# Mixer of layer 0: from a hand-braided order to recording and list scheduling

## The chip, the cores and the metric

The kernel runs on one core of a Trainium2 chip. The metric is the device time of one execution in microseconds (us), lower is better; several executions are timed and the median stands. One further execution is recorded by the hardware profiler, and every row below is of that one.

## The reference, cut to what matters

A decoder trunk of two layers over 16 learned tokens followed by 1024 tokens of width 1024, in float32. Layer 0 mixes with an RWKV-7 recurrence beside a causal pooling; layer 1 with differential attention. The change is in layer 0's mixer.

```python
def rwkv_pool_mixer(h, w_in, ...):            # layer 0
    y = h @ w_in                              # 18 slices of 128 columns here
    ys = ys + (prev - ys) * mu                # shift by one token
    r, k, v, wd, ad, gd = split(ys)
    decay, a, g = ...                         # low-rank products of wd, ad, gd
    o = rwkv7_scan(r, decay, k, v, kk, a)     # 8 heads: S = S*w + sa kk' + v k',  o = S r
    o = (groupnorm(o) * ln_w + ln_b + bonus) * g
    z = pooled differences of u, times pool_w # 4 groups, windows 2, 4, 8, 16
    return concatenate([o, z]) @ w_out

for i in range(2):
    m = rwkv_pool_mixer(hn) if i == 0 else diff_attn_mixer(hn)
    h = h + rmsnorm(m, g[1])
    h = h + rmsnorm(sq_relu_mlp(rmsnorm(h, g[2])), g[3])
```

## The kernel before, in words

**Layout.** Channels lie on the 128 partitions, tokens along the free axis. Large products are done in three TensorE passes on a high and a low part of each operand (`mm3`, L217 to L219: high by high, low by high, high by low). The small matrices of the recurrence are plain float32.

**The pieces of mixer 0.** Two heads make a pair, so there are four pairs p = 0 to 3. The scan is done in 17 chunks of 64 tokens, one alone and then eight groups of two: nine groups for each pair.
- `project` (L1009 to L1024) makes one of 18 slices of the input projection, and writes it to memory (`yd`, L1015) through a queue.
- `prep` (L1138 to L1180) loads a pair's slices back (`yl`, `la`) and builds the operands of each chunk: `pk` in memory, `ldd` (the triangular part) and a bonus `bond`.
- `invert` (L1190 to L1219) inverts the unit triangular blocks of a pair, 68 of 32 x 32 at once: loads `li` from `ldd`, then 31 steps of two VectorE operations each (L1211, L1212, on `li`, `xi`, `tm`), then `xi` goes out to `xd` (L1215) and comes back as `ds` (L1218, L1219).
- `chain` runs the recurrence over the nine groups of a pair, each group from the state that the one before left. Per group: load `lt` from `pk` (L1234), masks on GpSimd (`bd`, L1236, L1239), float32 matmuls (L1244, L1248, L1252, L1259, L1260, L1270, L1271, L1274, L1276), ScalarE and VectorE between them. Each 256 or so columns of output are finished by `fin` (L1287 to L1296): a norm (one matmul, L1290), scales, a product on GpSimd (L1295), and a store to `ozd`, from which `loads` (L1334, split on L237 and L238) brings them back as operands of the output projection.
- `pool_group` (L1306 to L1327) is the pooling of one channel group.
- `early` (matmul triples into `pse`) is the part of the output projection (6 of its 8 weight slices) that only needs finished operands.
- `late` (L537 and others) is the rest of layer 0: remaining output projection, norm, MLP. It is a list of tasks that a scheduler, class `Flow`, puts in order.

**What sets the order.** Mixer 0 is written in seven stages (`PLAN`, L60); in a stage `braid` takes pieces from several generators in turn, at fixed rates. Each engine executes its instructions in that order and waits where an operand isn't there. Nearly all of the mixer's transfers are issued by one queue, SP, in the same order: one that waits holds all behind it. `Flow` knows a cost for each task, its engine, what it needs, and one shared memory bus; it ranks tasks by the longest path behind them and places at each step the one that can start soonest. Before, only `late` and the stages behind it are ordered so.

**Buffers.** Pools give out tiles in rotation: PSUM has two banks for `project` and `early`, two for the chain's products (`xs`, `qp`), one each for `prep`'s results (`sa`, `sb` share one), its norms, the chain's output `ob` and its state `sp`. `li` and `xi` have one buffer each; the state S three; `ft` in `fin` five; `yl` five.

The names that follow have the kernel's own lines.

Of the kernel before, what the change touches and what calls it, by code (L numbers as in the profile page):

```python
# [7 lines left out]
F32 = mybir.dt.float32  # L8
# [53 lines left out]

class Later:
# [12 lines left out]
class Flow:  # L76
# [6 lines left out]
    def add(self, eng, cost, fn, r, w, port=False, size=0, tail=0.0):  # L83
# [8 lines left out]
        i = len(self.tasks)  # L92
        self.tasks.append((eng, cost, fn, deps, port, size, tail))
        for x in r:
            self.read.setdefault(x, set()).add(i)
        for x in w:
            self.wrote[x] = i
            self.read[x] = set()

# [65 lines left out]

class Trunk:
# [18 lines left out]
    def nm(self, s):  # L185
        self.uid += 1
        return f"{s}{self.uid}"

# [24 lines left out]
    def mm3(self, ps, ws, xs, first=True, last=True):  # L213
        nc = self.nc
        n = len(ws)
        for i, ((wh, wl), (xh, xl)) in enumerate(zip(ws, xs)):
            nc.tensor.matmul(ps, wh, xh, start=(first and i == 0), stop=False)  # L217
            nc.tensor.matmul(ps, wl, xh, start=False, stop=False)  # L218
            nc.tensor.matmul(ps, wh, xl, start=False, stop=(last and i == n - 1))  # L219
# [151 lines left out]
    def ahead(self, l):  # L371
# [5 lines left out]
        n = self.lw_n = (768, 768, 1024, 1024) if l == 0 else (640, 640, 1024, 1024, 1024)  # L377
# [15 lines left out]

    def late_weight(self, l, i, ne):
        nc = self.nc
        raw = self.R[0][:, i % 2, :self.lw_n[i]]
        hi, lo = self.lw(i)
        nc.sync.dma_start(raw, self.lw_src(l, i))
        nc.scalar.copy(hi, raw)
        nc.vector.tensor_tensor(lo, raw, hi.bitcast(F32), op=ALU.subtract)  # L400

    def late(self, l, xs, part, hin, hmid, hout, pre, rsb):
# [619 lines left out]
    def yload(self, mt, a, b):  # L1022
        y = self.yp.tile([P, 320], F32, tag="yl", name=self.nm("yl"), bufs=5)
# [93 lines left out]
    def prep_group(self, p, g0, m, e, ys, la, bo):  # L1117
# [45 lines left out]
        sb = self.mps.tile([P, 2, 4, C], F32, tag="p", name=self.nm("sb"))  # L1163
        for i in range(m):
            nc.tensor.matmul(sa[:, i, 2:4], kbd[:, i], w4[:, i, 1:3], start=True, stop=True)
        for i in range(m):
            nc.tensor.matmul(sa[:, i, 0:2], bbd[:, i], w4[:, i, 1:3], start=True, stop=True)
        for i in range(m):
# [3 lines left out]
        nc.vector.tensor_tensor(sg[:, :m, 0:4:2], sa[:, :m, 0:4:2],  # L1172
                                cb[:, None, None, B_MA:B_MA + C].broadcast_to([P, m, 2, C]), op=ALU.mult)
        nc.scalar.copy(sg[:, :m, 1:4:2], sa[:, :m, 1:4:2])
# [15 lines left out]
    def invert(self, p):  # L1190
# [3 lines left out]
        li = pp.tile([ni, 32, 32], F32, tag="li", name=self.nm("li"), bufs=1)  # L1194
        x = pp.tile([ni, 32, 32], F32, tag="xi", name=self.nm("xi"), bufs=1)
# [27 lines left out]
    def chain(self, p):  # L1223
# [5 lines left out]
        for f0, f1 in ((0, 1), (1, 5), (5, 9), (9, 13), (13, 17)):  # L1229
            ob = self.ops_.tile([P, 2, 4 * C], F32, tag="o", name=self.nm("ob"))  # L1230
            for g0 in range(f0, f1, 2):
# [33 lines left out]
                for i in range(n):  # L1265
# [3 lines left out]
                    if gi:  # L1269
# [605 lines left out]
```

## Time and profile before

| | us |
|---|---|
| median of 3 runs | 2822.95 (2817.04 to 2824.75) |
| the profiled execution | 2818.43 |
| its span, first to last instruction | 2816.6 |
| mixer 0 behind its entry and low-rank products, in the span | about 82 to 677 |
| mean granted TensorE clock over the span | 0.968 |

The profile's rows are of three kinds. Windows give the busy time of each engine in a stretch; matmuls overlap, so a busy TensorE isn't at its peak. A timeline lists instructions (neighbours that are alike are joined) with their start, their length and, in brackets, the idle time ahead of them and what ended it. The chain of waits follows the end of a stretch back to what released it.  PE is TensorE, PEld its weight loads, DVE VectorE, ACT ScalarE, POOL GpSimd, SP the queue for transfers, and SPq its issues. Kernel lines are written L1244.

Four instants cut mixer 0: the first matmul of each pair's chain (`xs<-lt,bd` of L1244, the single group of each pair). I call the stretches S0 (82 to chain 0), S1 (chain 0 to chain 1), S2 (chain 1 to chain 2), S3 (chain 2 to chain 3), S4 (chain 3 to the last `fin`), and "the tail" what lies between the last `fin` (L1290) and the long row of matmuls of `late`.

### The profile page before, as it was taken

Reading aid. Unit: us, or ns where it says so; the run is one execution under the profiler, and the core shown is the slowest. Engines: PE = TensorE matmul, PEld = TensorE weight load, DVE = VectorE, ACT = ScalarE, POOL = GpSimd, SP = SyncE. Lnnn points to the kernel's source line nnn. Section 1 sums busy time; section 2 is a strip of 40 time slices with the busy share of each in tenths; the row PEclk is TensorE's granted clock in tenths of the full one; section 3 lists DMA queues with packets and bytes.
Section 4 is the critical chain, followed back from the end, with each engine's and each line's share of the span. In section 5 each row is a group of like instructions: output and inputs, shape, how many; then the busy total and the mean of one; then the engine's idle time right before and its main releaser. Section 6 shows DMA issues by size and latency. Waiting matters only on the chain.

```text
span 2816.6 us, 44581 instructions
## 1 busy us (share of the span) xinstructions
PE 2622.5 (93%) x16822; PEld 2374.0 (84%) x16822; DVE 2102.9 (75%) x3889; ACT 1321.8 (47%) x2719; POOL 309.5 (11%) x404
## 2 busy tenths in 40 slices
PE   7999787898999999999968999999889999999997
PEld 6989786787899999999957898998786788878877
DVE  6568768463787778887795888878638787778888
ACT  6564564433643335433343556565635333344342
POOL 1112224131000000000012223222000000000000
PEclk9999988899999999999988999999999999999998
DMA  4656557555423346443342222222243233453443
GB/s 176 212 181 192 183 157 226 152 172 190 145 80 143 149 172 229 152 144 110 115 135 68 65 65 61 78 66 64 76 146 135 112 149 139 184 201 135 150 157 120
DMA packets 182774, 393.29 MB, mean 140 GB/s; under 512 B 43648, under 2 KB 106496, under 8 KB 170144
## 3 DMA queue, kind: packets, MB, share of 16 engines
q1 hardware_dynamic: 155376, 350.27, 37.4%
q10 hardware_dynamic: 27184, 40.18, 4.0%
q8 instruction: 132, 2.16, 0.3%
q14 instruction: 82, 0.67, 0.1%
HBM read 241.24 MB, written 132.24 MB: 133 GB/s over the span
## 4 chain that ended last, share of the span: by engine, by line
PE 63%; DVE 9%; ACT 2%; issue 2%; DMA 1%; POOL 0%; DVEq 0%; ACTq 0%; SPq 0%; POOLq 0%
PE bank L537 46%; PE psq L217 2%; PE psq L218 2%; PE psq L219 2%; PE s L1615 1%; PE tr L1661 1%; PE s L1617 1%; ACT p L1634 1%; PE pse L217 1%; PE bank L579 1%; PE av L1687 1%; PE pse L218 1%; PE pse L219 1%; DVE ac L614 1%; DVE p L1647 1%
## 5 line engine op out<-in xcount | busy, mean ns | idle before, releaser
L537 PE MATMUL bank<-opa,wp 128*128 128x260 f32 (+1 forms) x3296 | 655.4, 319 | 6.9 <-DVE wp L628 3.3
L537 PEld LDWEIGHTS bank<-opa,wp 128*128 128x128 f32 x3296 | 516.2, 188 | 56.7 <-DVE wp L628 5.0
L537 PE MATMUL bank<-opb,wp 128*128 128x260 f32 (+1 forms) x1150 | 347.6, 323 | 3.0 <-DVE ac L847 3.0
L537 PE MATMUL bank<-opa,hh 128*128 128x260 f32 (+1 forms) x1112 | 239.7, 320 | 7.2 <-DVE hh L628 5.3
L537 PEld LDWEIGHTS bank<-opb,wp 128*128 128x128 f32 x1150 | 216.3, 188 | 22.2 <-ACT opa L870 3.4
L847 DVE TENSOR_TENSOR ac<-bank,ac 128x520 f32<-128x520 f32 (+1 forms) x256 | 171.1, 691 | 67.5 <-PE bank L537 65.3
L537 PE MATMUL bank<-opa,opb 128*128 128x260 f32 (+4 forms) x1168 | 207.4, 308 | 13.4 <-ACT opb L516 7.1
L537 PEld LDWEIGHTS bank<-opa,hh 128*128 128x128 f32 x1112 | 184.8, 190 | 23.6 <-DVE hh L628 5.8
L537 PEld LDWEIGHTS bank<-opa,opb 128*128 128x128 f32 x1168 | 169.9, 196 | 24.9 <-ACT opb L516 7.5
L537 PE MATMUL bank<-opb,hh 128*128 128x260 f32 (+1 forms) x616 | 179.8, 325 | 0.0
L627 ACT CAST wp<-raw 128x512 fp32r<-128x512 f32 (+1 forms) x138 | 80.4, 584 | 199.3 <-PE bank L537 191.0
L627 ACT CAST wp<-ss 128x512 fp32r<-128x512 f32 (+1 forms) x130 | 76.5, 589 | 166.4 <-PE bank L537 141.1
L217 PE MATMUL ps<-opa,whi 128*128 128x346 f32 (+1 forms) x432 | 145.0, 336 | 0.4 <-DVE yt L1009 0.4
L218 PE MATMUL ps<-opa,wlo 128*128 128x346 f32 (+1 forms) x432 | 143.6, 332 | 0.0
L219 PE MATMUL ps<-opa,whi 128*128 128x346 f32 (+1 forms) x432 | 142.2, 329 | 0.6 <-DVE opa L315 0.6
L1634 ACT ACTIVATE p<-s,m 128x272 f32<-128x272 f32 (+7 forms) x128 | 95.6, 751 | 86.3 <-DVE m L1630 84.4
L537 PE MATMUL bank<-opa,tt 128*128 128x260 f32 (+1 forms) x648 | 130.5, 318 | 2.2 <-DVE ac L847 2.0
L537 PEld LDWEIGHTS bank<-opb,hh 128*128 128x128 f32 x616 | 116.9, 190 | 10.0
L217 PE MATMUL psq<-opa,wp 128*128 128x346 f32 (+2 forms) x352 | 118.1, 335 | 4.4 <-DVE rp L302 2.6
L203 POOL TENSOR_TENSOR wpx<-raw,wp 128x1024 fp32r<-128x1024 f32 (+1 forms) x14 | 33.9, 2425 | 789.8 <-PE bank L537 745.6
L219 PE MATMUL psq<-opa,wp 128*128 128x346 f32 (+2 forms) x352 | 113.8, 323 | 0.0
L537 PE MATMUL bank<-opb,opb 128*128 128x256 f32 (+4 forms) x456 | 111.4, 307 | 1.4 <-DVE tt L593 1.4
(408 smaller groups left out, 6928.2 us busy)
## 6 DMA issues: line engine op xcount, KB each, us to landing
raw<-in_w_dram SPq DMA_DIRECT2D x64, 1024.0 KB, 5.0
hid<-ac SPq DMA_DIRECT2D x14, 1820.0 KB, 6.6
hid<-ac SPq DMA_DIRECT2D x14, 1792.0 KB, 7.0
hh<-hid SPq DMA_DIRECT2D x23, 1040.0 KB, 5.1
hh<-hid SPq DMA_DIRECT2D x23, 1024.0 KB, 5.3
pk<-sg ACTq DMA_DIRECT2D x32, 704.0 KB, 4.4
lt<-pk SPq DMA_DIRECT2D x32, 704.0 KB, 4.6
raw<-in_w_qkv_dram SPq DMA_DIRECT2D x24, 512.0 KB, 3.4
```

The source lines that it names most:

```text
L203: (lo or nc.gpsimd).tensor_tensor(lw[:, :n], raw[:, :n], hi[:, :n].bitcast(F32), op=ALU.subtract)
L217: nc.tensor.matmul(ps, wh, xh, start=(first and i == 0), stop=False)
L218: nc.tensor.matmul(ps, wl, xh, start=False, stop=False)
L219: nc.tensor.matmul(ps, wh, xl, start=False, stop=(last and i == n - 1))
L537: nc.tensor.matmul(ps, use(x), use(y), start=start and i == j == 0, stop=i == len(ws) - 1 and j == 2, skip_group_check=not start)
L579: nc.tensor.matmul(acc, ones, use(src), start=first, stop=last)
L614: F.dve(NH, lambda mk=mk, k=k: stt(mk, mk, self.gcol(l, 1, k), y, op0=ALU.mult, op1=ALU.mult), r=nm + [("T", 2)], w=nm)
L627: F.act(n, lambda: nc.scalar.copy(use(t[0][:, :n]), src), r=rd, w=[z[0]] + claim)
L847: F.dve(NH, lambda d=d, q=q: tt(sv(d), q, sv(d), op=ALU.add), r=nq + nd, w=nd, ps=True)
L1615: nc.tensor.matmul(out(a, b), st[:, qs], kh[:, a:b], start=True, stop=False)
L1617: nc.tensor.matmul(out(a, b), st[:, qs], kl[:, a:b], start=False, stop=x1 <= x0)
L1634: nc.scalar.activation(p[:, :L0], S[c][:, :L0], AF.Exp, bias=m2[:, c:c + 1], scale=0.125, accum_out=m2[:, 2 + c:3 + c])
```

## The change

- Between the low-rank products and the end of mixer 0, `self.nc` is a `Recorder`: each call is kept with its engine, a cost, the memory regions that it reads and writes, and so its predecessors. At the end `rec.flow.run()` orders all with `Flow` and emits them. `PLAN` and `braid` still set the order of recording, and so which use of a buffer comes before which.
- A transfer is reckoned by packets: 8 ns and 0.0367 ns per byte for each contiguous run, over 16 engines, and .38 us of SP's time to issue it. GpSimd's operations and VectorE's of two operands outside PSUM are reckoned to exclude each other (`port`).
- Pools become `Ring`s of fixed tiles in rotation. The three matmuls of a triple, and the pairs that accumulate into `ob` and `sp`, are kept together (`group`).
- `li` and `xi` lie in `R[0]`, the raw buffer that `late` uses; it now exists from the mixer's start. At the mixer's end the raw weights 0 and 1 of the output projection are loaded into it, and cast in `late`'s list. Before, a function of its own did both ahead of the last stage.
- Pairs 2 and 3 split the output of `fin` directly into operands; there is no store to `ozd` and no load back.
- Smaller: S in two buffers, `ft` in four, `yl` in six; `sa` is read before `sb` is computed; `pool_group` uses two tiles in turn; some of the buffers of the next stages are allocated behind the mixer.

```diff
+class Ring:
+    def tile(self, shape, dtype, tag=None, name=None, bufs=None):
+        ...
+        ring[0] += 1
+        t = ring[1][(ring[0] - 1) % n][:, :free]
+        ...
+class Recorder:
+    def call(self, eng, op, args, kw):
+        ...
+        n = max(math.prod(int(k) for k in x.shape[1:]) for x in aps)
+        psum = any(x.space == PSUM for x in aps)
+        if op.startswith("dma"):
+            cost = 1.0 if eng == "POOL" else .38
+            words = math.prod(int(k) for k in out.shape)
+            run = min(self.run_of(x) for x in aps)
+            size = words / run * (8 + .0367 * 4 * run) / 16e3 * 350e3
+        elif eng == "PE":
+            cols, x = math.prod(int(k) for k in args[0].shape[1:]), args[1]
+            if x.dtype == F32R:
+                cost = max(cols / 2400 + .014, .108)
+            elif x.dtype == F32:
+                cost = 2 * max(2 * cols / 2400 + .003, .111)
+            ...
+        elif eng == "DVE":
+            cost = n / 960 + .07 + (.06 if psum else 0.0)
+        elif eng == "ACT":
+            wide = not psum and max(len(x.shape) for x in aps) > 2
+            cost = n / (1700 if psum else 1200) + (.2 if wide else .1) + (.08 if hasattr(kw.get("scale"), "ap") else 0.0)
+        else:
+            cost = n / 450 + .15
+        ...
+        port = eng == "POOL" or eng == "DVE" and not psum and len(aps) > 2
+        ...
@@ mm3
-            nc.tensor.matmul(ps, wh, xh, start=(first and i == 0), stop=False)
...
+            with self.group():
+                nc.tensor.matmul(ps, wh, xh, start=(first and i == 0), stop=False)
...
@@ late
-            if l or i > 1:
+            if True:
                 z = ("R", i % 4 // 2, i % 2)
                 raw = R[i % 4 // 2][:, i % 2, :n[i]]
-                F.dma(lambda raw=raw, i=i: nc.sync.dma_start(raw, self.lw_src(l, i)), n[i] * 512, w=[z])
+                if l or i > 1:
+                    F.dma(lambda raw=raw, i=i: nc.sync.dma_start(raw, self.lw_src(l, i)), n[i] * 512, w=[z])
@@ invert
-        li = pp.tile([ni, 32, 32], F32, tag="li", name=self.nm("li"), bufs=1)
-        x = pp.tile([ni, 32, 32], F32, tag="xi", name=self.nm("xi"), bufs=1)
+        li, x = [self.R[0][:ni, i].rearrange("p (a b) -> p a b", a=32) for i in (0, 1)]
@@ chain, fin
-            self.ozq.dma_start(self.ozd[4 + p, :, a - PAD:b - PAD], d)
+            if p < 2:
+                self.ozq.dma_start(self.ozd[4 + p, :, a - PAD:b - PAD], d)
+            else:
+                for c, (t0, W) in enumerate(self.quarters):
+                    u, v = max(a - PAD, t0), min(b - PAD, t0 + W)
+                    if u < v:
+                        self.split(d[:, u + PAD - a:v + PAD - a], v - u, [y[:, u - t0:v - t0] for y in self.xq(c, 4 + p)], nc.vector)
@@ mixer 0
+            rec = Recorder(tc)
+            self.nc = nc = rec
...
-                    for items in PLAN[:-1]:
-                        stage(items)
...
-                for i in (0, 1):
-                    self.late_weight(0, i, 6)
-                stage(PLAN[-1])
-                for _ in self.loads(xs, self.ozd, (6, 7), 0, 4):
-                    pass
+                for items in PLAN:
+                    stage(items)
+                for c, x in enumerate(xs):
+                    x += [self.xq(c, k) for k in (6, 7)]
+                self.late_x = xs
+                self.lw_n = LW[0]
+                for i in (0, 1):
+                    nc.sync.dma_start(self.R[0][:, i, :self.lw_n[i]], self.lw_src(0, i))
+                rec.flow.run()
```

How it moves instructions, at three places. All recorded instructions have line L283 of the changed kernel, so names tell what they are; a number such as `_0` behind a name is the tile of a ring.

SP before, around the loads of chain 1's second and third group (`lt<-pk` of 128 x 1408; the first, 128 x 704, stands 40 rows ahead). `li<-ldd` belongs to inversion 2.

```order
L1203 DMA li_4358<-ldd 16x32x32
L1204 DMA li_4358<-ldd 1x32x32
L1296 DMA ozd<-ft_4403 128x16
L1024 DMA yl_4487<-yd 128x256
L1015 DMA yd<-yt_4553 128x346
L1015 DMA yd<-yt_4581 128x346
L1306 DMA u_4675<-yd 128x364
L1234 DMA lt_4729<-pk 128x1408
L1015 DMA yd<-yt_4615 128x396
L1015 DMA yd<-yt_4644 128x346
L1234 DMA lt_4845<-pk 128x1408
```

SP now, the first of these loads (`lt_1`; the next stands seven rows behind it). `raw<-in_eye` fills inversion 2's `xi`; `xd<-raw` and `ds<-xd` are inversion 1's way out and back.

```order
L283 DMA xd<-raw_724 64x1024
L283 DMA xd<-raw_724 4x1024
L283 DMA ft_1_815<-gd 128x256
L283 DMA yd<-yt_0_768 128x346
L283 DMA raw_0_761<-in_wo_dram 128x768
L283 DMA la_3_781<-thd 128x256
L283 DMA ds_1_796<-xd 32x16x32 x4
L283 DMA lt_1_799<-pk 128x1408
L283 DMA raw_724<-in_eye_dram 64x1024
L283 DMA raw_724<-in_eye_dram 4x1024
```

The load moved ahead of inversion 2's own loads to a place beside inversion 1's way back; in the rows shown one store of `yd` and no `li<-ldd` stand ahead of it, where there were two of each.

VectorE before, the first operation of chain 2 that reads a product of the chain (`x<-lt,xs` of 128 x 128). The first step of inversion 3 stands 27 rows behind it.

```order
L1172 TENSOR_TENSOR sg_750<-sa_5703,conb 128x2x2x64
L238 TENSOR_TENSOR opa_70<-ho_5740,opa_70 128x260
L1175 TENSOR_TENSOR sg_750<-sb_5704,conb 128x2x192
L1250 TENSOR_TENSOR x_5923<-lt_5913,xs_5918 128x128
L302 SCALAR_TENSOR_TENSOR ft_5653<-ob_5502,ft_5653 128x256
L303 SCALAR_TENSOR_TENSOR ft_5655<-ft_5653,ft_5655 128x256
```

VectorE now, the same operation (`x_0<-lt_0,xs_0`).

```order
L283 TENSOR_TENSOR tm_0_794<-raw_724 68x60
L283 TENSOR_TENSOR raw_724<-raw_724,tm_0_794 68x30x2
L283 TENSOR_TENSOR tm_0_794<-raw_724 68x31
L283 TENSOR_TENSOR raw_724<-raw_724,tm_0_794 68x31
L283 TENSOR_TENSOR x_0_807<-lt_0_798,xs_0_803 128x128
L661 TENSOR_TENSOR opb_6261<-raw_724,opb_6261 128x768
L283 TENSOR_TENSOR qq_0_809<-lt_0_798,xs_1_804 128x128
```

All 62 operations of inversion 3 now stand ahead of chain 2.

TensorE before, the end of chain 3: `qp`, `sp` and `ob` are the chain's own, `ob<-ft` is the norm of the last `fin`, `bank` is `late`.

```order
L1259 MATMUL qp_7061<-lt_7043,gb_756 128x128
L1260 MATMUL qp_7061<-lt_7043,gb_756 128x128
L1274 MATMUL sp_7072<-lt_7043,mk_758 128x128
L1276 MATMUL sp_7072<-S_7013,mk_758 128x128
L1270 MATMUL ob_6973<-qq_7068,S_7013 128x64
L1271 MATMUL ob_6973<-qq_7068,lt_7043 128x64
L1270 MATMUL ob_6973<-qq_7068,S_7075 128x64
L1271 MATMUL ob_6973<-qq_7068,lt_7043 128x64
L1290 MATMUL ob_6973<-ft_7081,conb 128x256
L537 MATMUL bank_7412<-opa_71,opb_6522 128x260 x3
```

TensorE now, a piece in the midst of chain 3: `ps<-opa,whi` and `ps<-opa,wlo` of 128 x 260 are the triples of `early`.

```order
L283 MATMUL ps_0_766<-opa_73,whi_1_763 128x260
L283 MATMUL ob_0_797<-qq_1_810,S_0_812 128x64
L283 MATMUL ob_0_797<-qq_1_810,lt_0_798 128x64
L283 MATMUL ob_0_797<-qq_1_810,S_1_813 128x64
L283 MATMUL ob_0_797<-qq_1_810,lt_0_798 128x64
L283 MATMUL xs_0_803<-x_0_805,bd_0_801 128x128 x2
L283 MATMUL ps_1_767<-opa_74,whi_1_763 128x260
L283 MATMUL ps_1_767<-opa_74,wlo_1_765 128x260
L283 MATMUL ps_1_767<-opa_74,whi_1_763 128x260
L283 MATMUL ps_0_766<-opa_76,whi_1_763 128x260
L283 MATMUL ps_0_766<-opa_76,wlo_1_765 128x260
L283 MATMUL ps_0_766<-opa_76,whi_1_763 128x260
```

336 matmuls of `early` now stand behind chain 3's first one, the last 33 of them behind the last `fin`; before it was 150, and none behind the last `fin`. Counted so, the matmuls of each stretch stand as follows (chain, `prep`, `project`, `early`, `pool`), with the operations of VectorE and GpSimd in it:

| | S0 | S1 | S2 | S3 | S4 |
|---|---|---|---|---|---|
| before | 0, 200, 820, 0, 0 | 151, 105, 163, 0, 6 | 154, 101, 95, 20, 6 | 157, 6, 0, 262, 0 | 154, 0, 0, 150, 0 |
| now | 0, 200, 864, 0, 1 | 154, 103, 153, 0, 5 | 154, 109, 63, 12, 5 | 154, 0, 0, 84, 1 | 154, 0, 0, 336, 0 |
| now, VectorE | 418 | 248 | 325 | 74 | 65 |
| now, GpSimd | 62 | 53 | 59 | 23 | 29 |

## Rows read from the trace of the kernel before

**Rows 1.** Windows: start:end length, PE PEld DVE ACT POOL busy, clock, DMA share, GB/s.

```profile
82.00:273.60 191.60, 183.59 (x1219) 177.63 (x1217) 136.62 (x400) 101.36 (x328) 34.47 (x84) 0.97 0.58 184
273.60:387.10 113.50, 97.47 (x676) 88.92 (x677) 85.86 (x257) 68.91 (x228) 34.50 (x54) 0.95 0.60 189
387.10:514.80 127.70, 102.28 (x647) 92.56 (x646) 92.34 (x261) 73.05 (x242) 46.62 (x65) 0.87 0.60 188
514.80:610.90 96.10, 84.82 (x591) 77.33 (x591) 52.02 (x132) 35.61 (x97) 22.71 (x26) 0.89 0.53 161
610.90:676.40 65.50, 60.39 (x461) 55.00 (x459) 26.35 (x61) 28.67 (x78) 17.60 (x21) 1.00 0.44 139
82.00:677.00 595.00, 529.12 (x3589) 491.95 (x3588) 393.18 (x1109) 307.59 (x973) 155.90 (x249) 0.94 0.57 177
```

**Rows 2.** Timeline of PE: first matmuls of chains 0 to 3, last fin.

```profile
273.55 0.49 PE L1244 MATMUL xs<-lt,bd 128*128 128x128 f32 x2 [0.84 <-POOL bd L1236]
388.58 0.39 PE L1244 MATMUL xs<-lt,bd 128*128 128x128 f32 x2
515.25 0.44 PE L1244 MATMUL xs<-lt,bd 128*128 128x128 f32 x2
611.50 0.38 PE L1244 MATMUL xs<-lt,bd 128*128 128x128 f32 x2
676.43 0.70 PE L1290 MATMUL ob<-ft,conb 128*128 128x256 f32 x2 [0.47 <-ACT ft L1289]
```

**Rows 3.** Timeline of PE: neighbours of project, of early, of the chain.

```profile
89.68 0.32 PE L217 MATMUL ps<-opa,whi 128*128 128x346 f32 x1
89.84 0.32 PE L218 MATMUL ps<-opa,wlo 128*128 128x346 f32 x1
...
564.79 0.28 PE L219 MATMUL pse<-opa,whi 128*128 128x260 f32 x1
564.91 0.28 PE L217 MATMUL pse<-opa,whi 128*128 128x260 f32 x1
...
566.49 0.39 PE L1260 MATMUL qp<-lt,gb 128*128 128x128 f32 x2
566.71 0.39 PE L1259 MATMUL qp<-lt,gb 128*128 128x128 f32 x2
```

**Rows 4.** Timeline of SP, 400 to 432, and of PE at 435.

```profile
405.47 0.38 SPq L1024 DMA_DIRECT2D yl<-yd  x1
419.29 2.36 SPq L1015 DMA_DIRECT2D yd<-yt  x2
...
424.49 0.32 SPq L1234 DMA_DIRECT2D lt<-pk  x1
...
435.57 0.60 PE L1244 MATMUL xs<-lt,bd 128*128 128x128 f32 x4
```

**Rows 5.** Chain of waits, 195 to 760: chain 3's groups by their L1244.

```profile
625.15 0.45 PE xs L1244 x4
...
638.94 0.45 PE xs L1244 x4
```

**Rows 6.** Timeline behind the last fin.

```profile
679.10 6.02 PE L537 MATMUL bank<-opa,opb 128*128 128x260 f32 x33 [1.62 <-ACT opa L237]
...
690.15 9.97 PEld L537 LDWEIGHTS bank<-opa,opb 128*128 128x128 f32 x67 [0.98 <-DVE opb L517]
```

**Rows 7.** Timeline of POOL and DVE at 395, 410 and 641.

```profile
395.62 0.74 POOL L1295 TENSOR_TENSOR ft<-ft,ft 128x256 f32<-128x256 f32 x1
395.69 0.81 DVE L1160 TENSOR_TENSOR w<-q,q 128x128 f32<-128x128 f32 x1 [0.36 <-POOL q L1159]
410.32 0.29 DVE L1160 TENSOR_TENSOR w<-q,q 128x128 f32<-128x128 f32 x1 [0.57 <-POOL q L1159]
640.87 0.42 DVE L1264 TENSOR_TENSOR qq<-lt,qp 128x256 f32<-128x256 f32 x1
640.89 0.74 POOL L1239 TENSOR_TENSOR bd<-lt,conb 128x256 f32<-128x256 f32 x1 [3.57 <-DMA lt<-pk]
```

More of the change, by code (lines that the diff above doesn't have):

```diff
@@ L1399, in pools @@
                         yield from self.pool_group(g)
-                with tc.tile_pool(name="pp", bufs=6, reuse_waits="tile") as self.pp:
-                    self.rwkv_tiles()
-                    for _ in proj(*(4, 0, 8)[1:]):
-                        pass
-                    xs = [[] for _ in self.quarters]
-                    rest = self.early(xs, A["wo_0"], part, 6, 6)
-                    make = {"prep": self.prep, "invert": self.invert, "chain": self.chain, "proj": lambda a: proj(*a), "pool": lambda a: pools(*a),
-                            "load": lambda a: self.loads(xs, self.ozd, a, 0, 4), "early": lambda n: itertools.islice(rest, n)}
-                    stage = lambda items: self.braid([(make[kind](arg), rate) for kind, arg, rate in items])
-                    for items in PLAN[:-1]:
-                        stage(items)
@@ L1418, in mixer0 @@
-                self.ahead(0)
-                for i in (0, 1):
-                    self.late_weight(0, i, 6)
-                stage(PLAN[-1])
-                for _ in self.loads(xs, self.ozd, (6, 7), 0, 4):
-                    pass
-                self.late_x = xs
+                self.rwkv_tiles()
+                for _ in proj(*(4, 0, 8)[1:]):
+                    pass
+                xs = [[] for _ in self.quarters]
+                rest = self.early(xs, A["wo_0"], part, 6, 6)
+                make = {"prep": self.prep, "invert": self.invert, "chain": self.chain, "proj": lambda a: proj(*a), "pool": lambda a: pools(*a),
+                        "load": lambda a: self.loads(xs, self.ozd, a, 0, 4), "early": lambda n: itertools.islice(rest, n)}
@@ new lines, in mixer0 @@
+                stage = lambda items: self.braid([(make[kind](arg), rate) for kind, arg, rate in items])
+                for items in PLAN:
[4 more added lines that the diff above has]
+                self.lw_n = LW[0]
+                for i in (0, 1):
+                    nc.sync.dma_start(self.R[0][:, i, :self.lw_n[i]], self.lw_src(0, i))
+                rec.flow.run()
@@ L1425, in mixer0 @@
+            self.nc = tc.nc
+            self.wp, self.yp = entered
+        pool = self.base.enter_context(tc.tile_pool(name="base", bufs=1, side="right", reuse_waits="tile"))
+        self.WP = [pool.tile([P, 2, 512], F32R, name=self.nm("wp")) for _ in range(3)]
+        self.rsp = contextlib.ExitStack()
+        self.rsa = self.rsp.enter_context(tc.tile_pool(name="rsp", bufs=1, side="right", reuse_waits="tile")).tile([P, T], F32, name="rsa")
+        self.ahead(0)
         self.yp = None
```

170 lines of the change are left out of this document (134 added, 36 removed).

## The prediction, made before the changed kernel ran

> **What bounds the kernel now.** Only mixer 0 is touched, so I read its 595 us first, by windows, one for each stretch between the first matmuls of the chains [rows 1, 2]. Five stretches of 191.6, 113.5, 127.7, 96.1 and 65.5 us; their ends are fixed by the marks [rows 2]. The busy times alone mislead, since TensorE's matmuls overlap: in S1 it is busy 97.47 of 113.5 us. So I price its work by the pace of neighbours where it runs freely [rows 3]: starts 0.157 us apart in `project` (89.68 to 89.84), 0.118 in `early` (564.79 to 564.91), 0.222 for a float32 matmul of the recurrence, which leaves two records (566.49 to 566.71). With the matmuls counted for each stretch in the part on the change, the work before is 173.1, 86.0, 77.5, 67.1 and 51.9 us (S1: 256 of the recurrence's at .222, 163 of `project` at .157, 6 of `pool` at .6). That is .90 of the time in S0, but .76, .61, .70 and .79 in S1 to S4. VectorE is busy .71, .76, .72, .54 and .40 of the same stretches [rows 1]. No engine is full behind S0: the mixer is bound by waits in the order, and that is what a list schedule can move.
>
> Two places show it. SP: behind the load at 405.47 it issues nothing until 419.29, 13.4 us, a store of `yd` standing in front of chain 1's second `lt<-pk`, which then starts at 424.49 and is used at 435.57 [rows 4]; chain 1 had begun at 388.58 [rows 2]. So 47 us pass between its first and second group, while a group in chain 3 takes 6.9 us: 625.15 to 638.94 is two groups [rows 5]. And in S4 the last chain has little beside it, 150 matmuls of `early`, 17.7 us; it is bound by its own steps. The granted clock shows the gaps too: 0.87 and 0.89 in S2 and S3, where TensorE waits most, 1.00 in S4 [rows 1].
>
> **The change part by part.** What it removes: the store to `ozd` and load back for pairs 2 and 3, and the fixed braid. What it adds: a direct split of the same output, and the waits of fixed rings. What it moves: everything in the order. I price the new order by its work for each stretch, and a filling.
>
> *TensorE's work now*, same prices: S0 200 x .222 + 864 x .157 + .6 = 180.6; S1 154 + 103 at .222, 153 at .157, 5 at .6 = 84.1; S2 72.7; S3 154 x .222 + 84 x .118 + .6 = 44.7; S4 154 x .222 + 336 x .118 = 73.8, of which 33 matmuls (3.9) stand behind the last `fin`. *VectorE's work now*: 1109 operations took 393.18 us [rows 1], .3545 each; so S1 248 x .3545 = 88, S2 325 x .3545 = 115 (inversion 3 lies there now, ahead of chain 2), S3 26, S4 23. In S1 and S2 VectorE becomes the longest engine, not TensorE.
>
> *Filling.* S0 before is at .90; a list schedule takes what is ready, so I take .92 for a stretch that one engine bounds, with .97 as the best end (S0's TensorE is busy 183.59 of 191.6, .96) and, as the worst, what the order before gave, .76 and less.
>
> *S0*: 180.6/.92 = 196, so chain 0 starts at 82 + 196 = 278 (before 273.6: 44 matmuls more stand here now). *S1*: 88/.92 = 96, to 374. *S2*: 115/.92 = 125, to 499. *S3*: neither engine is full (44.7 and 26), so the chain's own steps set it: 9 groups. 6.9 us for a group [rows 5] has some 17 matmuls of `early` in it (150/9, 2.0 us), and 84/9 now, 1.1; if all of these lie in the way a group is 6.0, if none 6.9; I take 6.5, 58.5 us, to 558. *S4*: TensorE 69.9 ahead of the last `fin`, /.92 = 76, longer than the chain's 58.5, to 634. Before, the last `fin` was at 676.43 [rows 2]: **-42 us**.
>
> *SP's queue.* Chain 1's second load now stands behind inversion 1's way back, not behind inversion 2's way in. The chain needs inversion 1 anyhow, so I count no hold. If the store that is still ahead of it waits as before, the price is the 47 less one group's 6.5, some 40: a rival below. `Flow` reckons .38 us for each issue and packets for each transfer, so SP is not overfilled by its own sum; the DMA share of 0.58 to 0.60 in S0 to S2 [rows 1] leaves room when the same bytes go through 10% less time.
>
> *The tail.* Before, 13.7 us lie between the last `fin` (676.43) and the long row (690.15), with 33 matmuls of `late` among them; the row waits for VectorE's `opb`, a raw weight that was loaded late [rows 6]. Now weights 0 and 1 are cast during chain 2 and 33 matmuls of `early` lie behind the last `fin`; the round trip through `ozd` is gone; but the third weight still comes from a load of `late`. Gain at most 13.7 - 6.7 (676.43 to 679.10, and the 33 at .118 = 3.9) = 7, loss at most the 3.9 of the 33. I take 0.
>
> *Edits priced at nothing.* S in two buffers: ScalarE's copy of a state may now wait for the output matmuls of two chunks before; they are a few matmuls earlier on TensorE and hide it. Without that cover it costs one matmul, .222, for each of 68 chunks: 15 us over the mixer, 7.5 of it in S3 and S4. `ft` four, `yl` six, `sa` ahead of `sb`, two tiles in `pool_group`: each wants a product already made; S1 and S2 are filled by VectorE's inversions meanwhile. `li` and `xi` in the raw buffer were single before too. The stages behind the mixer keep their order but for its first casts.
>
> *GpSimd and VectorE.* A product on VectorE of two operands that are not in PSUM took 0.81 us at 395.69 while GpSimd ran for 0.74 from 395.62, and 0.29 at 410.32 with GpSimd idle; one that reads PSUM took 0.42 at 640.87 with GpSimd busy from 640.89 [rows 7]. So such an operation waits for GpSimd's end, .5 us here. The mean of .3545 holds such waits of before; inversions packed more densely beside GpSimd's work could meet more. The Trainium skill, "SBUF — State Buffer", section "SBUF: two separate sides", says that VectorE and GpSimd arbitrate for one pair of ports as an exclusive lock, held for a whole instruction, when VectorE has two inputs in SBUF. This trace agrees (0.81 against 0.29, and 0.42 undisturbed). By that rule the sum of both engines counts where their work is of this kind, which is the slower rival below; by the rows as they stand the sum stays at -42.
>
> *Sum.* On the profiled execution, 2818.43 - 42 = 2776. Its time is 4.5 us below the median, 2822.95; from the median it would be 2781. I take 2779, between.
>
> **The rivals.** *A, better filled.* At .97 in S0, S1, S2 and S4, and 5 us for a group in S3 (its matmuls, 154 x .222 / 9 = 3.8, and little between): 186 + 91 + 119 + 45 + 72 = 513, the last `fin` at 595, -82: 2737 to 2741. For it: S0's .96 busy. Against it: no row shows a group below 6.0.
>
> *B, SP still holds.* A store of `yd` or `ozd` in front of chain 1's or chain 2's loads waits for its engine, and a queue in order cannot pass it: +40 to +44, the last `fin` at about 676, time 2818 to 2825, no change. For it: 405.47 to 419.29 [rows 4] is just that. Against it: the scheduler places a store when its data are ready by its own sum.
>
> *C, slower: the two engines add up.* GpSimd's work in S1 and S2 is 53 + 59 operations at 155.90/249 = .626 us, 70 us [rows 1]. If VectorE's waits for it are wholly added to the 203 us there, S1 is 121 and S2 152 with no gap left, and the last `fin` is at 278 + 121 + 152 + 58.5 + 76 = 686, +9: 2828 on the profiled execution, 2832 from the median; with the gaps of .92 beside them it would be 634 + 70 = 704, +28. It decides once more than 42 of the 70 us are added to the forecast's 634, which is then at 676. Against it: operations that read PSUM are not held [rows 7], and in S2 before VectorE and GpSimd together were busy 92.34 + 46.62 = 139 us in 127.7 [rows 1], so they do overlap.
>
> *D, the change doesn't do what it says.* The order shows that it does: inversion 3 ahead of chain 2, `early` beside chain 3. No chance of its own.
>
> **How the numbers follow.** The forecast .59, A .20, B .11, C .10. About 0.3%, 8.5 us, is what a measurement of this kernel can tell from no change. Faster by more: the forecast and A, .79. Within: B, .11. Slower: C, .10. The range leaves out C, and some of A where it scatters to the faster side: from 2737, A's end, to 2826, B's end with a microsecond to spare; it also takes in the 15 us of S, the tail's -7 to +4 and a filling between .85 and .97.
>
> **What would show each step right or wrong.** Chains 0 to 3 begin at about 278, 374, 499 and 558, the last `fin` is near 634, the long row of `late` some 13 us behind it. VectorE is busy over .9 of S1 and S2. No gap of 10 us between two issues of SP ahead of an `lt<-pk`. Clock at 0.95 or above in S2 and S3. Behind the mixer the stretches keep their lengths. I am wrong if VectorE's operations without PSUM are near .6 us each in S1 and S2 (C), if a group in S3 takes 7 us or more, or if S1 or S2 has a gap of tens of microseconds with every engine idle (B).

## The result, and the profile after

The changed kernel takes 2804.41 us (2799.53 to 2807.09) against 2821.8 before: ratio 0.9939, interval 0.9928 to 0.9951, 17 us less. Forecast were 42 less: the direction was right, the size was not, and the time lies inside the range. The profiled execution took 2802.57 us, with a span of 2800.8.

Windows of the changed kernel, the five stretches from 82 to the last `fin` (columns as in [rows 1]):

```profile
82.00:288.10 206.10, 191.51 (x1267) 185.01 (x1267) 142.26 (x404) 111.03 (x348) 34.00 (x93) 0.98 0.57 181
288.10:392.00 103.90, 93.86 (x679) 87.41 (x678) 84.34 (x261) 71.90 (x230) 36.32 (x55) 0.98 0.68 217
392.00:522.80 130.80, 90.10 (x613) 81.26 (x612) 100.77 (x307) 74.25 (x239) 45.88 (x64) 0.85 0.65 197
522.80:588.30 65.50, 54.71 (x395) 50.61 (x395) 34.80 (x94) 31.35 (x88) 16.62 (x23) 0.86 0.53 156
588.30:660.30 72.00, 71.66 (x609) 71.14 (x608) 27.61 (x64) 31.21 (x89) 19.19 (x23) 1.00 0.41 128
```

| us | S0 | S1 | S2 | S3 | S4 | last `fin` |
|---|---|---|---|---|---|---|
| before | 191.6 | 115 | 127 | 96 | 65 | 676 |
| forecast | 196 | 96 | 125 | 58.5 | 76 | 634 |
| after | 206.1 | 103.9 | 130.8 | 65.5 | 72.0 | 660 |

Only S4 is better than forecast, and it is full: TensorE 71.66 of 72.00. S0 to S3 together take 30 us more than forecast. Behind the last `fin` nothing changed. Timeline of TensorE there, answering to [rows 6]:

```profile
660.12 0.60 PE L283 MATMUL ob<-ft,conb 128*128 128x256 f32 x2
...
666.01 3.86 PE L681 MATMUL bank<-opa,opb 128*128 128x260 f32 x30 [0.93 <-ACT yt L283]
672.57 0.39 PE L681 MATMUL bank<-opa,opb 128*128 128x260 f32 x1 [2.69 <-ACT opb L660]
673.82 16.36 PE L681 MATMUL bank<-opa,opb 128*128 128x260 f32 x119 [0.87 <-DVE opb L661]
```

From 660.12 to the long row at 673.82 are 13.7 us, as before (676.43 to 690.15): the tail of 0 was right, and the row still waits for the third weight.

**The hole ahead of chain 2.** Timeline of TensorE, all its matmuls from 494.48 to 530.29:

```profile
494.48 0.38 PE L283 MATMUL pss<-sr,conb 128*128 128x128 f32 x2
506.95 0.58 PE L283 MATMUL ps<-opa,whi 128*128 128x260 f32 x1 [12.08 <-ACT opa L283]
507.33 0.42 PE L283 MATMUL ps<-opa,wlo 128*128 128x260 f32 x1
510.39 0.59 PE L283 MATMUL ps<-opa,whi 128*128 128x260 f32 x1 [2.64 <-DVE opa L283]
519.49 0.58 PE L283 MATMUL ps<-opa,whi 128*128 128x260 f32 x1 [8.51 <-ACT opa L283]
519.87 0.42 PE L283 MATMUL ps<-opa,wlo 128*128 128x260 f32 x1
522.41 0.59 PE L283 MATMUL ps<-opa,whi 128*128 128x260 f32 x1 [2.12 <-DVE opa L283]
522.79 0.63 PE L283 MATMUL xs<-lt,bd 128*128 128x128 f32 x2
523.78 0.79 PE L283 MATMUL xs<-x,bd 128*128 128x128 f32 x2 [0.35 <-DVE tm L283]
530.29 0.77 PE L283 MATMUL xs<-lt,bd 128*128 128x128 f32 x2 [5.71 <-issue]
```

For 35 us TensorE has almost nothing, and chain 2's first matmul (522.79) stands behind triples of `early` that wait for splits (`opa`), which wait for their loads from `ozd`. What the other engines did, in their timelines:

```profile
486.29 1.00 SPq L283 DMA_DIRECT2D xd<-raw  x2
...
490.98 5.03 SPq L283 DMA_DIRECT2D raw<-ldd  x4
...
498.57 2.42 SPq L283 DMA_DIRECT2D raw<-ldd  x4
501.03 2.23 SPq L283 DMA_DIRECT2D ds<-xd  x4
...
505.21 0.45 POOL L283 TENSOR_TENSOR bd<-ds,conb 128x128 f32<-128x128 f32 x1 [5.69 <-DMA ds<-xd]
...
502.57 0.19 DVE L283 TENSOR_TENSOR tm<-raw 68x31 f32<-68x31 f32 x1 [5.10 <-DMA raw<-ldd]
...
529.79 0.21 DVE L283 TENSOR_TENSOR raw<-raw,tm 68x31 f32<-68x31 f32 x1
529.91 0.27 DVE L283 TENSOR_TENSOR x<-lt,xs 128x128 f32<-128x128 f32 x1
```

Inversion 2 goes out at 486.29, and the mask made of it is ready at 505.66: a round trip of 19 us. More than half of it is SP's order: by the chain of waits the way out had landed at 489.97, but SP issued inversion 3's way in (`raw<-ldd`) first, and inversion 2's way back (`ds<-xd`) only at 501.03. VectorE then does all of inversion 3, 502.57 to 530, and only behind it chain 2's `x` (529.91). From 502 to 522 VectorE is busy 18.16 of 20 us, TensorE 2.19, at a granted clock of 0.50, its lower level of 1.2 GHz.

### The profile page after: what moved, and what is told of

Same layout as the page of the kernel before. It is cut to its first block, busy times and chain, and to the rows that moved or that the text cites. A ratio compares the mean times of both kernels' runs of the same rounds, so it can differ in the third digit from the quotient of the medians.

```text
span 2800.8 us, 44525 instructions
## 1 busy us (share of the span) xinstructions
PE 2597.9 (93%) x16822; PEld 2359.1 (84%) x16822; DVE 2097.3 (75%) x3897; ACT 1332.5 (48%) x2727; POOL 302.4 (11%) x404
## 4 chain that ended last, share of the span: by engine, by line
PE 66%; DVE 9%; ACT 3%; issue 2%; DMA 2%; SPq 0%; POOL 0%; DVEq 0%; ACTq 0%
PE bank L681 46%; PE psq L368 2%; PE psq L369 2%; PE psq L370 2%; PE ps L283 2%; PE s L1777 1%; PE xs L283 1%; PE s L1779 1%; PE tr L1823 1%; ACT p L1796 1%; PE bank L723 1%; PE ob L283 1%; PE av L1849 1%; DVE p L1809 1%; DVE ac L758 1%
## 5 line engine op out<-in xcount | busy, mean ns | idle before, releaser
L283 PE MATMUL ps<-opa,whi 128*128 128x346 f32 (+2 forms) x1008 | 267.9, 328 | 31.9 <-ACT opa L283 20.6
L283 PEld LDWEIGHTS ps<-opa,whi 128*128 128x128 f32 x1008 | 179.5, 191 | 34.5 <-ACT opa L283 21.1
L283 PE MATMUL ps<-opa,wlo 128*128 128x346 f32 (+2 forms) x504 | 157.8, 313 | 0.0
L681 PE MATMUL bank<-opa,tt 128*128 128x260 f32 (+1 forms) x648 | 130.8, 319 | 2.2 <-ACT opb L1014 2.0
```

The source lines that it names most:

```text
L283: one = eng, cost, lambda: fn(*args, **kw), r, w
L681: nc.tensor.matmul(ps, use(x), use(y), start=start and i == j == 0, stop=i == len(ws) - 1 and j == 2, skip_group_check=not start)
```

## The experiments

**Theories.** *Order*: the list schedule carries the gain; *edits*: the direct split and the rings do. For the miss, *full engines* (the prediction's: VectorE bounds S1 and S2, TensorE S0) against *small waits* (the order is fixed by a plan whose waits are shorter than the chip's, and each engine then waits in order). For the hole, *starved masks* (the planner's exclusion of GpSimd and VectorE) against *round trip* (inversion 2's way out and back).

The marks of all runs, read from their timelines as in [rows 2]; the times are medians, the ratios go against the kernel before, and the marks are of the one profiled execution:

| run | time | ratio, interval | S0 | S1 | S2 | S3 | S4 |
|---|---|---|---|---|---|---|---|
| after | 2804.4 | .9939 (.9928 to .9951) | 206 | 104 | 131 | 65 | 72 |
| e1_recorded | 2816.5 | .9982 (.9969 to .9995) | 192 | 110 | 131 | 98 | 61 |
| e2_noport | 2797.2 | .9927 (.9905 to .9949) | 220 | 107 | 99 | 80 | 72 |
| e3_tie | 2792.2 | .9904 (.9888 to .9921) | 204 | 104 | 118 | 65 | 74 |
| e4_lat | 2769.9 | .9823 (.9807 to .9839) | 201 | 102 | 96 | 72 | 72 |
| e5_lat_port | 2786.8 | .9881 (.9865 to .9897) | 205 | 102 | 117 | 63 | 75 |
| e6_same | 2785.9 | .9879 (.9860 to .9898) | 206 | 102 | 108 | 65 | 75 |
| e7_ozd | 2806.4 | .9952 (.9935 to .9968) | 210 | 102 | 114 | 78 | 72 |
| e8_small | 2792.7 | .9908 (.9888 to .9928) | 202 | 101 | 127 | 61 | 72 |
| e9_pess | 2762.9 | .9796 (.9777 to .9816) | 191 | 101 | 93 | 74 | 75 |
| e10_seam | 2803.3 | .9938 (.9922 to .9955) | 203 | 103 | 135 | 67 | 72 |
| e11_bytes | 2822.0 | 1.0000 (.9989 to 1.0011) | 221 | 107 | 120 | 75 | 73 |
| e12_seam_lat | 2765.1 | .9801 (.9785 to .9816) | 197 | 103 | 96 | 72 | 72 |
| e13_seam_pess | 2758.9 | .9779 (.9762 to .9795) | 188 | 100 | 92 | 75 | 78 |
| e14_pess2 | 2778.0 | .9847 (.9826 to .9869) | 176 | 113 | 96 | 76 | 89 |
| e15_onepass | 2777.9 | .9845 (.9826 to .9864) | 183 | 101 | 133 | 63 | 72 |

### What carries the gain: e1, e7, e11

e1, the order of the framework instead of `Flow`'s:

```diff
-                rec.flow.run()
+                for t in rec.flow.tasks:
+                    t[2]()
```

> The recorded calls are emitted in the order of recording and the framework orders them, as in the kernel before; rings, direct split, inversion in the raw buffer and all the rest of the change stay. If the list schedule carries the gain, the last fin goes back to 670 to 690 and the time to 2812 to 2835. Rival: the gain comes from the direct split and the buffers, not from the order: 2798 to 2808, as the changed kernel (2804).

The framework, too, places instructions by itself where no order is given, as it did before the change. 2816.5, a ratio of .9982: the edits are worth about 5 us, the list schedule the other 12. S3 shows it: 98 us without the schedule, 65 with it.

e7 puts the store to `ozd` and the loads back for pairs 2 and 3:

```diff
-            if p < 2:
+            if True:
...
-                for c, x in enumerate(xs):
-                    x += [self.xq(c, k) for k in (6, 7)]
+                for _ in self.loads(xs, self.ozd, (6, 7), 0, 4):
+                    pass
```

> The direct split of pairs 2 and 3 is undone: their output goes to memory and back, as before, all still list-scheduled. By the prediction the split is worth the tail alone, 0 to 7 us: 2804 to 2812. Rival: it is a main part of the gain, since the order of recording alone gave 4 us: 2812 to 2822. Third: nothing, 2800 to 2806.

2 us slower, within what can be told apart. S2 is 17 us shorter and S3 13 longer; the list only laid inversion 3 elsewhere.

e11 takes the transfers' costs from the later stages' lists:

```diff
-            cost = 1.0 if eng == "POOL" else .38
-            words = math.prod(int(k) for k in out.shape)
-            run = min(self.run_of(x) for x in aps)
-            size = words / run * (8 + .0367 * 4 * run) / 16e3 * 350e3
+            cost = .06
+            size = 4 * math.prod(int(k) for k in out.shape)
```

> The changed kernel with transfers reckoned as in the later stages' lists: bytes over the bus alone and .06 us to issue. If packets and SP's .38 us matter, SP is overfilled by its plan, and loads that engines wait for come late: 2812 to 2830. Rival: the plan is bound elsewhere: 2798 to 2808.

2822.0, as slow as before: with transfers reckoned so, the list schedule gains nothing. S0 alone is 15 us longer. Whether the packets or SP's .38 us do it, this run doesn't tell.

### Full engines or small waits: e8, e15, e6, e4

e8 has the order of the changed kernel, with short operations in the inversions: each is planned as it stands and issued on what `small` holds.

```diff
+            nc.small = tv[:, :1], li[:, j:j + 1, j + 1:].broadcast_to([ni, 1, a]), x[:, :1, j:j + 1].broadcast_to([ni, 1, a])
             E.tensor_tensor(tv, ...)
+            nc.small = x[:, :1, j + 1:], x[:, :1, j + 1:], tv[:, :1]
             E.tensor_tensor(x[:, :m, j + 1:], x[:, :m, j + 1:], tv, op=ALU.subtract)
```

> The order of the changed kernel, instruction for instruction, but the 62 VectorE operations of each inversion work on the first column of the inverse alone, at most 31 elements, so that each takes some 0.1 instead of 0.375 us: 16 us less for an inversion; the other columns of the inverses stay undone. By the prediction VectorE bounds S1 and S2: S1 16 us shorter, S2 30, the time 2755 to 2765. Rival, latencies: only where the inversion stands alone, the hole ahead of chain 2, something goes, 10 to 25 us: 2780 to 2795.

e15 has the same order, with one matmul of each recorded triple of `project`; the products of the low parts are left out:

```diff
-            self.keep(..., [c[2] for c in calls], ...)
+            self.keep(..., [c[2] for c in (calls[:1] if self.cut else calls)], ...)
```

> The order of the changed kernel, but of each recorded triple of project only the first matmul is issued, so that TensorE has 90 us less to do in S0, 16 in S1, 7 in S2; the products of the low parts are left out of the projection. By the prediction S0 is TensorE's: it falls until VectorE's 142 us stop it, 145 to 165 us. S1: if it is TensorE's work with small waits on top, 85 to 92; if latencies of the recurrence's steps, 97 to 104, as with shortened inversions (101).

Windows of S1 in e8 and of S0 and S1 in e15:

```profile
283.90:385.20 101.30, 93.21 (x678) 87.19 (x677) 74.22 (x260) 71.40 (x230) 32.95 (x54) 0.98 0.69 218
```

```profile
82.00:265.00 183.00, 127.02 (x690) 111.31 (x691) 141.26 (x403) 109.97 (x347) 34.55 (x93) 0.84 0.64 203
265.00:365.50 100.50, 85.03 (x576) 75.52 (x574) 83.03 (x258) 71.09 (x229) 33.77 (x54) 0.93 0.68 215
```

VectorE has 10 us less to do in S1 of e8 (74.22 for 84.34), and S1 is 2.6 us shorter. TensorE has 16 us less in S1 of e15 (two thirds of 153 matmuls at .157), and S1 is 3.4 shorter; it has 90 us less in S0, and S0 is 23 shorter, at a clock of 0.84 instead of 0.98. So neither engine by itself sets S1; that the two hold it in turn is not excluded, since no run takes work from both. In S0 TensorE's work counts in part, a quarter of what was taken away. *Full engines* falls as the prediction had it, one engine's work over .92. The order itself is what both kept.

The hole gets 7 us shorter in e8 (28, from 488.5 to 516.4), with 17 us less for VectorE in S2 (83.64 for 100.77): VectorE's splits stand in the midst of inversion 3, and they wait for loads from `ozd`.

What is left for the hole are the waits between the steps, and what stands ahead of what. Two pairs of neighbours on VectorE in the changed kernel's timeline, independent at 163, dependent at 529:

```profile
163.73 0.28 DVE L283 SCALAR_TENSOR_TENSOR q<-q,q 128x128 f32<-128x128 f32 x1
163.93 0.28 DVE L283 TENSOR_TENSOR w<-yl,pw 128x128 f32<-128x128 f32 x1
...
529.30 0.22 DVE L283 TENSOR_TENSOR raw<-raw,tm 68x60 f32<-68x60 f32 x1
529.55 0.21 DVE L283 TENSOR_TENSOR tm<-raw 68x31 f32<-68x31 f32 x1
```

The first starts 0.20 us ahead of the next, as the planner's cost has it (128/960 + .07). The dependent one, with 60 elements, is planned at 0.13 and starts 0.25 ahead. The planner lets a dependent step on the same engine start at once; here it comes 0.12 us later. In an inversion that is 62 times, 7 us: 15.7 us by the planner's costs are 23, and with splits between them 27, at 502.57 to 530. e6 tells the planner just that:

```diff
-                ready[j] = max(ready[j], end + (0.0 if T[j][0] == e and not size else .3))
+                ready[j] = max(ready[j], end + (self.same.get(e, 0.0) if T[j][0] == e and not size else .3))
...
+                rec.flow.same = {"DVE": .12, "ACT": .135}
```

> The changed kernel, the planner told of one thing alone: a dependent operation on the same engine starts 0.12 (VectorE) or 0.135 us (ScalarE) later. Theory, dependent operations: this is most of the slip of S0 to S2, and since it also leaves gaps at the port between the steps of an inversion, it ends the starving of the masks: 2768 to 2788. Rival: the gain came from transfers reckoned 0.8 us longer: 2797 to 2806.

2785.9, 18 us less than the changed kernel: two constants give as much again as the whole change. All of it is in S2 (131 to 108); S0 and S1 stay at 206 and 102.

### The hole: e2, e3, e4, e5

e2 drops the exclusion:

```diff
-        port = eng == "POOL" or eng == "DVE" and not psum and len(aps) > 2
+        port = False
```

> In the changed kernel the planner's rule that GpSimd and two-operand VectorE operations exclude each other is dropped for mixer 0. Theory, starved masks: by that rule GpSimd's masks of chain 2 (bd<-ds) come behind all of inversion 3, since VectorE wins every tie for the port, and the splits and early stand in the way; without it chain 2's first VectorE step comes at 505 to 512 instead of 530, and 15 to 25 us go: 2779 to 2790. Rival, round trip: chain 2 waits for inversion 2's way out and back, which ends at 505 to 507 in any order, and VectorE must do inversion 3 anyhow: 2800 to 2808. Third: GpSimd and VectorE now collide on the chip more than the planner knows, and it gets slower than 2812.

e3 keeps it, and changes the tie:

```diff
-                if best is None or lo < best[0]:
+                if best is None or lo < best[0] or self.tie and lo == best[0] and rank[i] > rank[best[2]]:
```

> The exclusion stays in the planner, but of two engines that could start at the same instant the one with the longer path behind it goes first, instead of VectorE always ahead of GpSimd. Starved masks: 10 to 22 us less, 2782 to 2795, chain 2's first VectorE step before 520. Round trip: 2800 to 2808.

e4 is e2 with e6's edit and 2.8 for 2.0 us behind a transfer's bytes; e5 is e3 with the same numbers:

```diff
-                end = bus + 2.0
+                end = bus + self.lat
...
+                rec.flow.same, rec.flow.lat = {"DVE": .12, "ACT": .135}, 2.8
```

> As without the exclusion, and the planner is told what the trace of the changed kernel shows: an operation of VectorE that needs the one just ahead of it starts 0.12 us later than the planner has it, one of ScalarE 0.135; a transfer takes 2.8 instead of 2.0 us beyond its bytes. Theory, latencies: S0 and S1 run 15 to 20 us later than planned because small waits add up in a fixed order; an order that knows them takes another 10 to 25 us: 2758 to 2780. Rival: the slip comes from work that no order can hide (clock, full engines): as without the exclusion, 2779 to 2790.

> The planner knows the measured latencies, as in the run with latencies and without the exclusion (2770), but keeps the exclusion of GpSimd and two-operand VectorE operations, with ties to the longer path. If the exclusion is real on the chip and only the tie was wrong, the order fits better: 2752 to 2766. Rival: the exclusion costs the plan more than it tells: 2768 to 2785.

Timeline of e3 where inversion 3 begins, GpSimd, TensorE and VectorE:

```profile
504.24 0.19 DVE L283 TENSOR_TENSOR tm<-raw 68x31 f32<-68x31 f32 x1 [1.85 <-DMA raw<-ldd]
...
507.21 0.45 POOL L283 TENSOR_TENSOR bd<-ds,conb 128x128 f32<-128x128 f32 x1 [4.22 <-DMA ds<-xd]
507.71 0.80 PE L283 MATMUL xs<-lt,bd 128*128 128x128 f32 x2 [6.73 <-POOL bd L283]
510.72 0.29 DVE L283 TENSOR_TENSOR x<-lt,xs 128x128 f32<-128x128 f32 x1 [3.40 <-PE xs L283]
```

With ties to the longer path chain 2's `x` comes at 510.72, not 529.91, in the midst of inversion 3: *starved masks* is right for the second half of the hole, and 12 us go. It is a matter of the plan: on the chip the mask was ready at 505.66 in the changed kernel too, and waited for engines that the plan had sent elsewhere. The first half is the *round trip*, which stays: `bd` waits for `ds` until 507. e2 fell between its two ranges. It takes 31 us from S2, but S0 is 13 longer, S1 4 and S3 14, so that the last `fin` is at 660 as in the changed kernel; its profiled execution (2805.9) was the slowest of its four, and where the median's 7 us lie the marks don't show. Where the plan drops the exclusion, more than the hole moves. e4, the same without the exclusion but with the latencies, goes to 2769.9, 27 us below e2 by the medians; S0 alone is 19 shorter. Its timeline shows inversion 2 going out 20 us earlier, and chain 2 right behind its return:

```profile
466.24 1.00 SPq L284 DMA_DIRECT2D xd<-raw  x2
...
472.55 1.47 SPq L284 DMA_DIRECT2D ds<-xd  x3
...
480.34 1.39 POOL L284 TENSOR_TENSOR bd<-ds,conb 128x128 f32<-128x128 f32 x2 [4.40 <-DMA ds<-xd]
481.11 0.49 PE L284 MATMUL xs<-lt,bd 128*128 128x128 f32 x2 [1.56 <-POOL bd L284]
482.59 0.28 DVE L284 TENSOR_TENSOR x<-lt,xs 128x128 f32<-128x128 f32 x1
```

The way back now stands ahead of inversion 3's `raw<-ldd` (482.74). What this place in SP's order is worth by itself no run tells.

e5 missed: with the exclusion the same latencies give 2786.8, 17 us more than without, S2 alone 21, although a VectorE operation does wait for GpSimd on the chip [rows 7]. So what the latencies are worth depends on the rest of the plan: 18 us in e6, 27 from e2 to e4, 5 from e3 to e5. Why the truer rule makes the worse order is open.

### Slack, and the start: e9, e14, e10, e12, e13

e9 is e4 with more: `hand` from engine to engine, `more` for each operation. e14 has .25, .28, 3.4, .7 and .08 instead:

```diff
+                rec.flow.same, rec.flow.lat, rec.flow.hand, rec.flow.more = {"DVE": .18, "ACT": .2}, 2.8, .5, .04
```

> Without the exclusion, and the planner told longer waits than the trace shows: 0.18 and 0.2 us for dependent operations, 0.04 us more for each operation of VectorE and ScalarE, 0.5 us from engine to engine, 2.8 us beyond a transfer's bytes. If the fixed order still loses by waits that come out longer than planned (2770 with the measured values), a plan with slack loses less: 2745 to 2764. Rival: the measured values are enough, and slack only shifts work: 2766 to 2785.

> Still more slack in the planner: 0.25 and 0.28 us for dependent operations, 0.08 us more for each operation of VectorE and ScalarE, 0.7 us from engine to engine, 3.4 us beyond a transfer's bytes. If small waits are what is left to be lost, 2750 to 2762. Rival: the plan is now wrong on the other side and the gain is used up: 2762 to 2780.

e9, with longer waits in the plan than e4, gets to 2762.9, and S0 is back at the 191 of before. Its window:

```profile
82.00:273.10 191.10, 178.56 (x1208) 174.64 (x1208) 135.61 (x408) 112.66 (x360) 33.86 (x91) 0.99 0.60 194
```

Of S0's 15 us some 10 are moved, not gained: 798 matmuls of `project` lie in it where the changed kernel has 864 (1208 records of matmuls for 1267), and 66 at .157 are 10.4 us. They come back later; S1 has 710 records for 679. e14 goes too far: S0 is shortest of all (176, with 138 matmuls of `project` fewer, 22 us), but S1 and S4 grow by 9 and 17 against the changed kernel, with 67 and 70 records more, and the time is 2778. So slack pays up to a point.

e10 begins to record two slices of `project` later; e12 does so on e4, e13 on e9:

```diff
-            rec = Recorder(tc)
-            self.nc = nc = rec
...
                 self.rwkv_tiles()
                 for _ in proj(*(4, 0, 8)[1:]):
                     pass
+                rec = Recorder(tc)
+                self.nc = nc = rec
```

> The changed kernel with two of the 18 slices of project (the first two behind the low-rank products) left out of the recording, so that the framework can put them among the low-rank products, as before. Theory, seam: S0 is 14.5 us longer than before because the recorded part can't begin ahead of its first instruction: 44 matmuls (6.9 us) that lay ahead of 82 and some 5 us of idle TensorE at half clock behind it; chain 0 begins at 273 to 280 instead of 288, the time is 2790 to 2797. Rival: S0 is long by the planner's latencies, and the start costs nothing: chain 0 at 284 or later, 2800 to 2807.

> Latencies, no exclusion, and the two slices outside of the recording: if the seam is its own cost, the two add up, 2755 to 2763 (2770 with latencies alone, less 7 to 14). If the latencies had already taken the seam in, 2766 to 2773.

> The plan with slack (2763) and the two first slices of project outside of the recording. If the seam's 5 us, as seen with the measured latencies (2770 to 2765), is there with slack too: 2754 to 2761. Rival: the plan with slack already begins S0 well (191 us, as before): 2761 to 2770.

The framework, where it orders by itself, had put `project` (L217 to L219) among the low-rank products (L1067); the recorded part can't begin ahead of its first instruction. Timeline of TensorE before, and windows from 82 to 102 before and after:

```profile
75.27 1.33 PE L1067 MATMUL psg<-lx,lw 128*128 128x346 f32 x4
76.18 0.58 PE L217 MATMUL ps<-opa,whi 128*128 128x348 f32 x1
...
77.08 0.74 PE L1067 MATMUL psg<-lx,lw 128*128 128x346 f32 x2
```

```profile
82.00:102.00 20.00, 20.00 (x128) 20.00 (x127) 10.79 (x22) 3.14 (x9) 4.52 (x12) 1.00 0.43 136
```

```profile
82.00:102.00 20.00, 15.13 (x78) 14.71 (x78) 9.40 (x26) 10.58 (x33) 5.03 (x17) 0.83 0.62 198
```

5 us idle and a clock of 0.83. e10 fills that window (TensorE busy 20.00, clock 1.00), but S0 is only 3.6 us shorter and S2 4 longer: 2803.3, no gain, the *seam* theory as expected there is wrong. The 44 matmuls that it puts ahead of 82 weren't there either: by the counts in the part on the change they came from S1 and S2, and e10's S0 holds as many records as the changed kernel's (1265 and 1267). On the better plans the medians fall by 4 to 5 us (e12 against e4, e13 against e9), less than the 8.5 that can be told apart; e12 lies between its two ranges, and the last `fin` is 2.6 and 0.9 us earlier. e13, 2758.9, has the lowest median, 2.2% under the kernel before and 1.6% under the changed one; e9's runs (2758.0 to 2769.4) overlap with it.

## Why the prediction was right or wrong, point by point

- **What bounds the kernel**: waits in the order, no full engine. Right for the kernel before, and then not held to: in S0 to S2 of the changed kernel I let one engine bound again.
- **Filling of .92: this step failed.** It came out at .88 in S0 (180.6 of 206.1), and at .85 and .88 in S1 and S2 by the work that I had put there (88 of 103.9, 115 of 130.8). In S1 and S2 I had VectorE bound; it is busy .81 and .77 there, not over .9, and the clock is 0.85 and 0.86 in S2 and S3, not .95. e8 and e15 show that taking work from either engine hardly shortens S1, and S0 by a quarter of what is taken. The time was not out of reach: e9's five stretches take 533.6 us, with no less work, where I had 552. What was missing, as far as the runs show it, is that this plan knows shorter waits than the chip has, and that I took a filling instead of asking what a fixed order does with them. The price: some 10, 8 and 6 us in S0, S1 and S2. That the planner's short waits are behind S2 is shown by e6 (131 to 108, by two constants). S0 is shown in part only: it stays at 206 in e6, e4 with the same matmuls takes 5 of the 10, the start (e10) 3.6, and of e9's 15 some 10 are matmuls that moved to later stretches. S1 is open: it takes 100 to 104 us in most runs, with the waits told or not, and with work taken from either engine; that dependent steps set it is only argued.
- **VectorE's price.** .3545 us for each operation was the mean over all; S2's operations are shorter, 100.77 us for 307 (.328), not 115 for 325.
- **Inversion 3 ahead of chain 2.** I read it from the order, and priced it as work in S2. It was a wait: 27 us of inversion and splits at the end of a round trip of 19, with TensorE empty and at half clock. e3 takes 12 us of it by letting chain 2's masks and `x` in between. The hold at SP that I counted at nothing is in it, too: inversion 2's way back stood 11 us behind inversion 3's way in (489.97 to 501.03). I had looked at chain 1's loads alone.
- **S3.** 6.5 us for a group was right (522.8 to 575.4 is eight, 6.6 each); the ninth, up to chain 3's first, took 12.9, which I had not counted. **S4**: fuller than .92, 72.0 for 76. **Tail**: 0, right to a tenth.
- **S in two buffers and the other edits at nothing**: not tried one by one; e1 holds them all, and is 5 us faster than before.
- **Rivals.** B: chain 1's second group now comes 5.9 us behind its first (before 47, [rows 2, 4]), so SP's hold there is gone, as forecast; one of 11 us came in ahead of chain 2. C: fell; S1 is at 104, not 121. A: not this order, but an order of this kind; e9's last `fin` is at 615.6, between the forecast's 634 and A's 595.
- **The rule on the shared port.** It was weighed as a reason for the slower rival. The trace after agrees with the wait (an inversion step of 68 x 156 took 0.85 us at 408.09, with GpSimd busy from 407.11 to 409.78, and 0.32 at 526.87, with GpSimd idle), but the weight lay elsewhere: not in the time that VectorE loses to GpSimd on the chip, but in what the planner does with the rule (e2, e3, e5).

## What to carry to other kernels

A list schedule becomes a fixed order, so a wait that its planner leaves out can be paid by all engines behind it; measure the start-to-start time of dependent neighbours, and put that in before pricing the new order by work. An order shows what stands ahead of what, and a stretch of one engine's work ahead of another's first step (an inversion ahead of a chain) should be priced as a wait, not as filling. To see whether an engine bounds a stretch, keep the order and take work from it: what doesn't shorten wasn't bound by it alone. And before a shorter stretch is called a gain, count what work was moved out of it.

## What the runs showed of the hardware

A VectorE operation that needs the result of the one just ahead starts 0.12 us later than the planner has it (0.25 against 0.13 at 529.30), while an independent one starts on time and 0.08 us ahead of its neighbour's end (0.20 at 163.73, of 0.28). The Trainium skill, "VectorE: DVE Perf Modes", section "The DRAIN you can't avoid", says that after every operation the next one does not start until the pipeline is empty, and adds that a next operation that is not held starts earlier. The trace agrees with both halves: the independent one starts before the end of its neighbour (0.20 behind its start, of 0.28), the dependent one behind it (0.25, of 0.22). An order that puts an independent operation between two dependent ones should gain by it.

The way of an inversion's result through memory and back took 19 us in the changed kernel and 14 in e4 (466.24 to 480.34). The transfers themselves are the smaller part: in the changed kernel 3.7 us out (486.29 to 489.97) and 4.2 from the first issue back to the mask's start (501.03 to 505.21); for the 11 us between them SP was at other transfers.
